# A gated linear unit over 8192 x 8192: two tiles to one store, and a load that waits for the tile before it

## The chip, the core and the metric

The kernel runs on one core of a Trainium2 chip. The metric is the device time of one execution in microseconds (us); the profile comes from one profiled execution, the times from separate ones. Transfers between HBM (the chip's large memory) and SBUF (the core's own memory of 128 partitions) are carried by 16 DMA engines, which serve the queues of all issuers: loads are issued by SyncE (SP), stores by ScalarE (ACT). VectorE (DVE), ScalarE and GpSimd (POOL) compute; TensorE has no work here.

## The reference

```python
# x: (8192, 8192) float32
a, b = np.split(x, 2, axis=-1)
return a * (1 / (1 + np.exp(-b)))     # (8192, 4096) float32
```

Of each row the first half is multiplied by the sigmoid of the second half. 268.4 MB are read and 134.2 MB written.

## The kernel before

**Tiles.** The 8192 rows are cut into 32 tiles of 256 rows. A tile puts R = 2 neighbouring rows into each of the 128 partitions: `x_g[i // 2, i % 2]` is a block in which partition p holds 2 x 8192 floats, 64 KB, that lie together in HBM. Two tiles with the same `i // 2` are interleaved: of four neighbouring rows the first two belong to the even tile, the last two to the odd one. So a tile's result is 2 x 4096 floats, 32 KB, in each partition, and the results of the two tiles of a pair together are 64 KB that lie together in HBM.

**Buffers.** SBUF has two slots for x (`xs`, 64 KB per partition each) and two for the result (`os`, 32 KB each); tile i uses slot `i % 2` of both.

**Work on a tile** (`work`). ScalarE writes sigmoid(b) over b in place (line 82); the product of a and that goes to the output slot (line 84). An ordinary tile is done in two pieces (`few_and_most`): 3/16 of the columns of both rows (1536 elements per partition), whose product is made by GpSimd, and the other 13/16 (6656 elements), whose product is made by VectorE. Tile 0 and tile 31 are done in four pieces of 2048 elements each (`fourths`), with products on VectorE alone, and tile 1 has both its products on VectorE.

**Order and waits.** The loop goes over the tiles: the two pieces of work, the load of tile i + 2, the store of tile i. Each engine runs its own instructions in this order. `place` drops every dependency on a tile's buffers but those named:

- a load waits for the products of the tile that had its x slot, two tiles back;
- a sigmoid waits for its load, and, in tiles 1 to 30, for the store that frees the output slot;
- a product waits for its sigmoid (in tile 31 for the freed output slot as well);
- a store waits for the products of its tile.

Tile 0 is loaded in two halves and stored in two halves; tile 31 is stored in pieces of a half, a quarter and a quarter. `_launch_early` puts the first load ahead of the start-up barrier, and `_close_on_sync` rewrites the end of the program so that only SyncE waits for the last store.

Of the kernel before, what the change touches and what calls it, by code (L numbers as in the profile page):

```python
# [8 lines left out]
def _tiles(ctx, tc, x, out):  # L9
    nc = tc.nc  # L10
    P = nc.NUM_PARTITIONS
    DEP = mybir.DependencyInfo(mybir.DependencyClass.Sync, mybir.DependencyReason.DATA)
    fp32 = mybir.dt.float32
    SIG = mybir.ActivationFunctionType.Sigmoid

    n_rows, n_cols = x.shape
    half = n_cols // 2
    R = 2
    SLOTS = 2
    n_tiles = n_rows // (P * R)  # L20
    x_g = x.rearrange("(g p h r) m -> g h p (r m)", p=P, h=2, r=R)
    out_g = out.rearrange("(g p h r) m -> g h p (r m)", p=P, h=2, r=R)

    pool = ctx.enter_context(tc.tile_pool(name="io", bufs=1))
    xs = [pool.tile([P, R * n_cols], fp32, name=f"x_sb{k}") for k in range(SLOTS)]
    os = [pool.tile([P, R * half], fp32, name=f"o_sb{k}") for k in range(SLOTS)]

    whole = [(0, 8)]
    rows = [(0, 4), (4, 8)]
    cut = half // 16 * 3  # L30
    few_and_most = [(0, 8, 0, cut), (0, 8, cut, half)]
    fourths = [(k, k + 2, k % 4 * half // 4, (k % 4 + 2) * half // 4) for k in range(0, 8, 2)]
    loads = [whole] * n_tiles
    works = [few_and_most] * n_tiles
    stores = [whole] * n_tiles
    behind = [0] * n_tiles
    loads[0] = stores[0] = rows
    works[0] = works[-1] = fourths
    stores[-1] = [(0, 4), (4, 6), (6, 8)]
    behind[-1] = 1  # L40

    def meet(a, b):
        return a[0] < b[1] and b[0] < a[1]

    traced = [[] for _ in range(SLOTS)]
    load_of, mul_of, store_of = {}, {}, {}

    def place(i, ins, *needs):


        kept = {n.ins.name for n in needs}
        for e in traced[i % SLOTS]:
            if e.ins.name not in kept:
                tc.declare_no_dep(ins.ins, e.ins, reason="follows from the waits that are kept")
        traced[i % SLOTS].append(ins)
        tc.keep_in_program_order(ins)
        return ins

    def load(i):
        for lo, hi in loads[i]:  # L60
            c = slice(lo * n_cols // 4, hi * n_cols // 4)
            free = [m for w, m in mul_of.get(i - SLOTS, []) if meet(w, (lo, hi))]
            ins = nc.sync.dma_start(out=xs[i % SLOTS][:, c], in_=x_g[i // 2, i % 2, :, c])  # L63
            load_of.setdefault(i, []).append(((lo, hi), place(i, ins, *free)))

    def store(i, lo, hi):
        c = slice(lo * half // 4, hi * half // 4)
        ins = nc.scalar.dma_start(out=out_g[i // 2, i % 2, :, c], in_=os[i % SLOTS][:, c])  # L68
        done = [m for w, m in mul_of[i] if meet(w, (lo, hi))]
        store_of.setdefault(i, []).append(((lo, hi), place(i, ins, *done)))  # L70

    def work(i, lo, hi, near, far):

        rows = xs[i % SLOTS].rearrange("p (r h m) -> p r h m", r=R, h=2)
        packed = os[i % SLOTS].rearrange("p (r m) -> p r m", r=R)
        r, c = slice(lo // 4, (hi + 3) // 4), slice(near, far)
        b = rows[:, r, 1, c]
        landed = [s for w, s in load_of[i] if meet(w, (lo, hi))]
        gone = [s for w, s in store_of.get(i - SLOTS, []) if meet(w, (lo, hi))]
        by_sigmoid = 0 < i < n_tiles - 1  # L80
        needs = [*landed, *(gone if by_sigmoid else ())]
        sig = place(i, nc.scalar.activation(out=b, in_=b, func=SIG), *needs)  # L82
        engine = nc.gpsimd if far == cut and i > 1 else nc.vector
        mul = engine.tensor_mul(out=packed[:, r, c], in0=rows[:, r, 0, c], in1=b)  # L84
        if by_sigmoid:
            for s in gone:
                tc.add_manual_dep(sig.ins, s.ins.name, DEP, reason="frees the output slot")
        place(i, mul, sig, *(() if by_sigmoid else gone))
        mul_of.setdefault(i, []).append(((lo, hi), mul))

    for i in range(SLOTS):
        load(i)
    for i in range(n_tiles):
        due = list(stores[i])
        for k, piece in enumerate(works[i]):
            work(i, *piece)
            ready = works[i][k - behind[i]][1] if k >= behind[i] else 0
            while len(stores[i]) > 1 and k < len(works[i]) - 1 and due[0][1] <= ready:
                store(i, *due.pop(0))
        if i + SLOTS < n_tiles:  # L100
            load(i + SLOTS)
        for lo, hi in due:
            store(i, lo, hi)


def _launch_early(nc):
# [68 lines left out]
@with_exitstack  # L175
def kernel(
    ctx: ExitStack,
    tc: tile.TileContext,
    x: bass.AP,
    out: bass.AP,  # L180
):
    nc = tc.nc
    with ExitStack() as pools:
        _tiles(pools, tc, x, out)
    tc.close()
    tc.compile()
    _launch_early(nc)
    _close_on_sync(nc)
# [30 lines left out]
```

## Time and profile before

| | before |
|---|---|
| median of 3 runs | 932.73 us (932.71 to 932.75) |
| profiled execution, first to last instruction (its span) | 931.1 us |
| between the span and the median | 1.6 us |
| VectorE busy | 232.5 us, 25% of the span, 39 multiplies |
| ScalarE busy | 229.8 us, 25%, 68 activations and a table load |
| GpSimd busy | 99.9 us, 11%, 29 multiplies and 4 memsets |
| sigmoids of an ordinary tile | 1.48 + 5.73 us |
| its products | GpSimd 3.44 us, VectorE 7.09 us |
| one load, issue to landing (median) | 43.5 us |
| one store, issue to landing (median) | 43.6 us |

The profiled execution's own time is its span of 931.1 us and what lies around it: the page gives no other time for it, and the runs stand 1.6 us above the span. In the profile's lines L63 is the load, L68 the store, L82 the sigmoid and L84 the product. In lines of the chain the columns are start, duration (both in us) and what ran; in the timeline they are start, busy time, engine, line, operation, buffers and shapes, count, and in brackets the idle time before it with what ended it; in a window they are the stretch, its length, the busy time of VectorE, ScalarE and GpSimd with their instructions, the TensorE clock, the share of the DMA engines and GB/s. Digits in the row of slices are tenths of a fortieth of the span, 9 being 90% or more.

### The profile page before, as it was taken

The numbers are of one execution on the slowest core, as the hardware profiler recorded it, in microseconds if no ns is written. First come the engines' busy times: TensorE is split into PE (matmuls) and PEld (weight loads), VectorE is DVE, ScalarE is ACT, GpSimd is POOL, SyncE is SP. The second block draws the span as 40 slices with busy tenths as digits, with TensorE's granted clock in tenths as the row PEclk, the third lists the DMA queues.
The fourth block names the chain that finished last, engine by engine and source line by source line (L and its number), as shares of the span: only waits on it lengthen the run. The fifth ranks groups of instructions, "written<-read, shape, count | busy, mean of one in ns | idle before, by whom it ended". The sixth has DMA issues, their size and how long they took to land.

```text
span 931.1 us, 325 instructions
## 1 busy us (share of the span) xinstructions
DVE 232.5 (25%) x39; ACT 229.8 (25%) x69; POOL 99.9 (11%) x33
## 2 busy tenths in 40 slices
DVE  1133311333113331133320333203332033320233
ACT  2123332033320333203332023320233302333023
POOL 0001111011110111101111011110111101111010
DMA  9999999999999999999999999999999999999998
GB/s 405 450 439 417 428 450 424 455 405 428 450 428 450 407 469 409 428 450 427 452 405 450 428 428 450 424 452 408 428 450 428 450 408 465 411 428 450 427 452 383
DMA packets 9793, 402.67 MB, mean 432 GB/s; under 512 B 1088, under 2 KB 1088, under 8 KB 1088
## 3 DMA queue, kind: packets, MB, share of 16 engines
q1 hardware_dynamic: 4752, 268.44, 66.6%
q10 hardware_dynamic: 5040, 134.22, 33.4%
q14 instruction: 1, 0.01, 0.0%
HBM read 268.44 MB, written 134.22 MB: 432 GB/s over the span
## 4 chain that ended last, share of the span: by engine, by line
DMA 75%; DVE 12%; ACT 12%; issue 0%; ACTq 0%; SPq 0%
DMA out_dram<-o_sb 65%; DVE o_sb L84 12%; ACT x_sb L82 12%; DMA x_sb<-in_x_dram 10%; ACTq L68 0%; SPq L63 0%
## 5 line engine op out<-in xcount | busy, mean ns | idle before, releaser
L84 DVE TENSOR_TENSOR o_sb<-x_sb 128x6656 f32<-128x6656 f32 (+2 forms) x39 | 232.5, 5970 | 690.2 <-ACT x_sb L82 690.2
L82 ACT ACTIVATE x_sb<-x_sb 128x1536 f32<-128x1536 f32 (+1 forms) x68 | 228.5, 3407 | 689.9 <-DMA out_dram<-o_sb 630.0
L84 POOL TENSOR_TENSOR o_sb<-x_sb 128x1536 f32<-128x1536 f32 x29 | 99.7, 3437 | 787.7 <-ACT x_sb L82 787.7
L82 ACT ACT_TABLE_LOAD x1 | 1.3, 1283 | 0.8 <-PEq L203 0.8
L203 POOL MEMSET const-float32-0.0<- 128x1 f32 x1 | 0.1, 98 | 0.2 <-issue 0.2
L203 POOL MEMSET const-bfloat16-1.0<- 128x1 bf16 x1 | 0.1, 101 | 0.0
L203 POOL MEMSET const-uint8-127<- 128x1 uint8 x1 | 0.1, 101 | 0.0
L203 POOL MEMSET const-float32-1.0<- 128x1 f32 x1 | 0.1, 98 | 0.0
## 6 DMA issues: line engine op xcount, KB each, us to landing
out_dram<-o_sb ACTq DMA_DIRECT2D x30, 4096.0 KB, 43.6
x_sb<-in_x_dram SPq DMA_DIRECT2D x2, 4096.0 KB, 16.4
out_dram<-o_sb ACTq DMA_DIRECT2D x3, 2048.0 KB, 28.0
out_dram<-o_sb ACTq DMA_DIRECT2D x2, 1024.0 KB, 8.3
x_sb<-in_x_dram SPq DMA_DIRECT2D x31, 43.5
```

Of the source, the lines that this page charges most:

```text
L82: sig = place(i, nc.scalar.activation(out=b, in_=b, func=SIG), *needs)
L84: mul = engine.tensor_mul(out=packed[:, r, c], in0=rows[:, r, 0, c], in1=b)
L203: nc = _bacc.Bacc("TRN2", target_bir_lowering=False, num_devices=1)
```

## The change

The two output slots become one buffer of 64 KB per partition (`packed`): the even tile writes its first half, the odd tile its second. Tiles 0 to 29 form 15 pairs, and each pair is written by one store of 64 KB per partition, issued after the odd tile's products. Tiles 30 and 31 keep stores of their own.

The waits change with it:

- the products of a pair's first tile wait for the store of the pair before, and so do those of tiles 30 and 31; no sigmoid waits for a store any more;
- the load of an odd tile from tile 3 on waits, besides the products that free its x slot, for the last sigmoid of the even tile before it; it is issued in that tile's turn, ahead of the load of the next even tile, which still waits for the products of the tile in its slot;
- tile 30's store is issued by itself, and tile 31's pieces follow as before: a half, a quarter, a quarter.

Pieces, engines and sizes of the computation stay. The core of the diff:

```diff
-    out_g = out.rearrange("(g p h r) m -> g h p (r m)", p=P, h=2, r=R)
+    out_g = out.rearrange("(g p k) m -> g p (k m)", p=P, k=2 * R)
...
-    os = [pool.tile([P, R * half], fp32, name=f"o_sb{k}") for k in range(SLOTS)]
+    packed = pool.tile([P, 2 * R * half], fp32, name="o_sb")
+    n_paired = n_tiles // 2 - 1
...
+    def is_paired(i):
+        return i < 2 * n_paired
...
+    def load(i, after=()):
+        for lo, hi in [(0, 4), (4, 8)] if i == 0 else [(0, 8)]:
             c = slice(lo * n_cols // 4, hi * n_cols // 4)
             ins = nc.sync.dma_start(out=xs[i % SLOTS][:, c], in_=x_g[i // 2, i % 2, :, c])
+            place(ins, mul_of.get(i - SLOTS, []), after)
             load_of.setdefault(i, []).append(((lo, hi), ins))
...
+    def store(i, lo, hi, done):
         c = slice(lo * half // 4, hi * half // 4)
+        ins = nc.scalar.dma_start(out=out_g[i // 2, :, c], in_=packed[:, c])
+        return place(ins, done)
...
-        sig = place(i, nc.scalar.activation(out=b, in_=b, func=SIG), *needs)
+        sig = place(nc.scalar.activation(out=b, in_=b, func=SIG), landed)
...
+        mul = place(engine.tensor_mul(out=o[:, r, c], in0=rows[:, r, 0, c], in1=b), [sig, *gone[i % 2]])
...
     for i in range(n_tiles):
+        first, last = i == 0, i == n_tiles - 1
+        for k, piece in enumerate(fourths if first or last else few_and_most):
             work(i, *piece)
+            if last and k == 2:
+                store(i, 8, 12, mul_of[i][:2])
+        if i % 2 == 0 and 0 < i + 1 - SLOTS:
+            if is_paired(i - 1):
+                load(i + 1, [sig_of[i][-1]])
+        if i + SLOTS < n_tiles and not (i % 2 and is_paired(i)):
             load(i + SLOTS)
+        if is_paired(i):
+            if i % 2:
+                s = store(i, 0, 16, mul_of[i - 1][-2:] + mul_of[i])
+                gone = [[s], [s]]
+            else:
+                gone[1] = []
+        elif not last:
+            gone[i % 2] = [store(i, i % 2 * 8, i % 2 * 8 + 8, mul_of[i])]
+    store(n_tiles - 1, 12, 14, mul_of[n_tiles - 1][2:3])
+    store(n_tiles - 1, 14, 16, mul_of[n_tiles - 1][3:])
```

More of the change, by code (lines that the diff above doesn't have):

```diff
@@ L21, in _tiles @@
     x_g = x.rearrange("(g p h r) m -> g h p (r m)", p=P, h=2, r=R)
-    out_g = out.rearrange("(g p h r) m -> g h p (r m)", p=P, h=2, r=R)
+    out_g = out.rearrange("(g p k) m -> g p (k m)", p=P, k=2 * R)
     pool = ctx.enter_context(tc.tile_pool(name="io", bufs=1))
     xs = [pool.tile([P, R * n_cols], fp32, name=f"x_sb{k}") for k in range(SLOTS)]
-    os = [pool.tile([P, R * half], fp32, name=f"o_sb{k}") for k in range(SLOTS)]
-    whole = [(0, 8)]
-    rows = [(0, 4), (4, 8)]
+    packed = pool.tile([P, 2 * R * half], fp32, name="o_sb")
+    n_paired = n_tiles // 2 - 1
     cut = half // 16 * 3
@@ L32, in _tiles @@
     fourths = [(k, k + 2, k % 4 * half // 4, (k % 4 + 2) * half // 4) for k in range(0, 8, 2)]
[L33 to L46, printed above, removed]
@@ L48, in place @@
-    def place(i, ins, *needs):
-        kept = {n.ins.name for n in needs}
-        for e in traced[i % SLOTS]:
+    def is_paired(i):
+        return i < 2 * n_paired
+    placed = []
+    sig_of, mul_of, load_of = {}, {}, {}
+    gone = [[], []]
+    def place(ins, needs, after=()):
+        kept = {n.ins.name for n in (*needs, *after)}
+        for e in placed:
             if e.ins.name not in kept:
                 tc.declare_no_dep(ins.ins, e.ins, reason="follows from the waits that are kept")
-        traced[i % SLOTS].append(ins)
+        for n in (*needs, *after):
+            tc.add_manual_dep(ins.ins, n.ins.name, DEP, reason="kept")
+        placed.append(ins)
@@ L56, in place @@
         tc.keep_in_program_order(ins)
         return ins
-    def load(i):
-        for lo, hi in loads[i]:
+    def load(i, after=()):
+        for lo, hi in [(0, 4), (4, 8)] if i == 0 else [(0, 8)]:
             c = slice(lo * n_cols // 4, hi * n_cols // 4)
-            free = [m for w, m in mul_of.get(i - SLOTS, []) if meet(w, (lo, hi))]
             ins = nc.sync.dma_start(out=xs[i % SLOTS][:, c], in_=x_g[i // 2, i % 2, :, c])
-            load_of.setdefault(i, []).append(((lo, hi), place(i, ins, *free)))
@@ L66, in store @@
-    def store(i, lo, hi):
+            place(ins, mul_of.get(i - SLOTS, []), after)
+            load_of.setdefault(i, []).append(((lo, hi), ins))
+    def store(i, lo, hi, done):
         c = slice(lo * half // 4, hi * half // 4)
-        ins = nc.scalar.dma_start(out=out_g[i // 2, i % 2, :, c], in_=os[i % SLOTS][:, c])
-        done = [m for w, m in mul_of[i] if meet(w, (lo, hi))]
-        store_of.setdefault(i, []).append(((lo, hi), place(i, ins, *done)))
+        ins = nc.scalar.dma_start(out=out_g[i // 2, :, c], in_=packed[:, c])
+        return place(ins, done)
@@ L72, in work @@
     def work(i, lo, hi, near, far):
         rows = xs[i % SLOTS].rearrange("p (r h m) -> p r h m", r=R, h=2)
-        packed = os[i % SLOTS].rearrange("p (r m) -> p r m", r=R)
+        o = packed.rearrange("p (h r m) -> p h r m", h=2, r=R)[:, i % 2]
         r, c = slice(lo // 4, (hi + 3) // 4), slice(near, far)
         b = rows[:, r, 1, c]
-        landed = [s for w, s in load_of[i] if meet(w, (lo, hi))]
-        gone = [s for w, s in store_of.get(i - SLOTS, []) if meet(w, (lo, hi))]
-        by_sigmoid = 0 < i < n_tiles - 1
@@ L81, in work @@
-        needs = [*landed, *(gone if by_sigmoid else ())]
-        sig = place(i, nc.scalar.activation(out=b, in_=b, func=SIG), *needs)
-        engine = nc.gpsimd if far == cut and i > 1 else nc.vector
[L84 to L89, printed above, removed]
+        landed = [s for w, s in load_of[i] if w[0] < hi and lo < w[1]]
@@ L91, in _tiles @@
+        sig = place(nc.scalar.activation(out=b, in_=b, func=SIG), landed)
+        engine = nc.gpsimd if far == cut and i > 1 else nc.vector
+        mul = place(engine.tensor_mul(out=o[:, r, c], in0=rows[:, r, 0, c], in1=b), [sig, *gone[i % 2]])
+        sig_of.setdefault(i, []).append(sig)
+        mul_of.setdefault(i, []).append(mul)
     for i in range(SLOTS):
@@ L93, in _tiles @@
     for i in range(n_tiles):
-        due = list(stores[i])
-        for k, piece in enumerate(works[i]):
+        first, last = i == 0, i == n_tiles - 1
+        for k, piece in enumerate(fourths if first or last else few_and_most):
             work(i, *piece)
[L97 to L100, printed above, removed]
-            load(i + SLOTS)
-        for lo, hi in due:
-            store(i, lo, hi)
+            if last and k == 2:
[4 more added lines that the diff above has]
+        if i + SLOTS < n_tiles and not (i % 2 and is_paired(i)):
+            load(i + SLOTS)
+        if is_paired(i):
[8 more added lines that the diff above has]
+    store(n_tiles - 1, 14, 16, mul_of[n_tiles - 1][3:])
 def _launch_early(nc):
```

## The prediction

> **What bounds the kernel now.** I read the page from the top: engines, then slices, then DMA queues.
>
> ```profile
> span 931.1 us, 325 instructions
> ...
> DMA  9999999999999999999999999999999999999998
> ...
> DMA packets 9793, 402.67 MB, mean 432 GB/s; under 512 B 1088, under 2 KB 1088, under 8 KB 1088
> ...
> q1 hardware_dynamic: 4752, 268.44, 66.6%
> q10 hardware_dynamic: 5040, 134.22, 33.4%
> ```
>
> The 16 DMA engines are busy in every slice; VectorE and ScalarE, the busiest engines, stand at 25% of the span. q1 (loads) and q10 (stores) add up to 100.0%, so bytes bound the kernel. The counts also give the packets: 33 loads of 128 rows are 4224, 16 small ones per load make 4752. The 35 stores give 4480 + 560 = 5040. So a load packet is one row of 64 KB, a store packet one of 32 KB.
>
> Next, the chain of waits over one tile, the timeline of the next, and one window of 29 us.
>
> ```profile
> 99.66 7.13 ACT x_sb L82 x2
> 106.79 0.02 issue
> 106.81 7.10 DVE o_sb L84
> ...
> 113.99 43.64 DMA out_dram<-o_sb
> 157.63 0.02 issue
> 157.66 7.13 ACT x_sb L82 x2
> ```
>
> ```profile
> 128.66 7.12 ACT L82 ACTIVATE x_sb<-x_sb 128x1536 f32<-128x1536 f32 x2 [21.88 <-DMA out_dram<-o_sb]
> 130.22 3.44 POOL L84 TENSOR_TENSOR o_sb<-x_sb 128x1536 f32<-128x1536 f32 x1 [25.56 <-ACT x_sb L82]
> 135.81 7.09 DVE L84 TENSOR_TENSOR o_sb<-x_sb 128x6656 f32<-128x6656 f32 x1 [21.91 <-ACT x_sb L82]
> 142.99 0.35 ACTq L68 DMA_DIRECT2D out_dram<-o_sb  x1
> ```
>
> ```profile
> 99.66:128.66 29.00, 7.09 (x1) 7.12 (x3) 3.44 (x1) 1.00 1.00 434
> ```
>
> A tile takes 29.0 us, in which 8.39 MB are loaded and 4.19 MB stored: 434 GB/s. The chain runs through stores, but a store's 43.6 us are queueing: 14.6 behind the store before it, 29.0 for itself. In the 29.0 us a load moves twice the bytes, so packets of 64 KB and of 32 KB alternate. Both queues always hold work, so nothing the compute engines do is seen. GpSimd's multiply ends at 133.66, VectorE's begins at 135.81: they never run together.
>
> **What the change moves.** Bytes and engine instructions stay the same; stores go from 35 to 19. The only possible gains are cheaper packets; the only losses are stretches with empty queues.
>
> *Fewer, longer store packets.* In the trace's packet records 64 KB take 2.418 us and 32 KB take 1.213 us, so joining two saves 2 x 1.213 - 2.418 = 0.008 us. Each engine joins 8 rows per pair, in 15 pairs: 120 x 0.008 = 0.96. Neighbouring packets overlap by a few ns, so I take 0.9 us of gain. Issue instructions saved (16 of 0.36 us) lie beside transfers: nothing.
>
> *Start and end.* The first store is issued some 37 us later (18.45 before, near 55.7 by the steps below), but loads fill that time. At the end only stores remain in both versions, with the same last piece sizes: nothing.
>
> *The new order in a pair.* Call the tiles A and B, the next pair's A' and B', then A''. One tile's load, alone, takes 8.39 MB / 434 GB/s = 19.3 us, and so does a pair's store. With 64 KB packets in both queues they now share by halves, not 2:1. "l" is the time from an issue to its first packet, taken as equal for every transfer. Count from B's last packet; A' is queued behind B:
>
> 1. B: landing 0.4 (last packet to sigmoid), sigmoids 7.13, multiply 7.10, issue 0.04: the store is issued at 14.7, first packet at 14.7 + l. A' then has 4.6 - l to go, and shares.
> 2. A' lands; sigmoids 0.4 + 7.13; only then is B' issued, first packet l later. The store runs alone for 7.5 + l and has 19.3 - (4.6 - l) - (7.5 + l) = 7.2 left. This is the cover of the new wait: the queues don't run dry there unless sigmoids and issue take 7 us more. Behind the waiting load on SP's queue stands only A'', which must wait longer anyway.
> 3. Store and B' share; the store ends 14.4 us later, and B' has 19.3 - 7.2 = 12.1 left. **These 12.1 us are all the cover there is.**
> 4. The multiplies of A' wait for the whole store, as they overwrite its buffer. A'' needs the x slot of A', so it waits for both multiplies. From the store's last packet: landing 0.6 (99.10 to 99.66 in the trace), VectorE 7.10, then l: 7.7 + l. If GpSimd's 3.44 us come on top: 11.2 + l. ACT's queue holds the store of the pair and behind it the sigmoids of a tile that lands later; GpSimd and VectorE hold B's multiplies behind A's, and B has not landed: no further loss.
>
> So the queues stand empty for c = 7.7 + x + l - 12.1 = x + l - 4.4, if positive. Two costs in it are shown by no row.
>
> x, the price of both multiplies being released by one store: between 0 and 3.44 us (the serial end). A gain is excluded: an operation gets no shorter by having company. I take 3.44: the nearest rows have the two strictly one after the other, both read the same x tile and write the same buffer, and no row shows a free overlap.
>
> The Trainium skill (SBUF — State Buffer, "Who interferes with whom") says that a VectorE instruction with two SBUF inputs and a GpSimd instruction that reads SBUF exclude each other for a whole instruction; by this rule x is 3.44 too and the sum is the one below. This trace has no overlap to test it on.
>
> l: the very first load shows its first packet 1.01 us after issue, with idle engines; the first store (issued at 18.45, first packet at 23.58) took 5.13 beside a running load. Those are the ends. Of the 5.13 one running packet of 2.42 may be waiting for a turn, which a load behind its own queue doesn't pay: I take 5.13 - 2.42 = 2.7.
>
> c = 3.44 + 2.7 - 4.4 = 1.7 us. An empty stretch delays A'' by as much, so more of it is shared with the next store, and the next cover grows by that stretch: the next gap is c minus this one. On average c/2. The loads of tiles 4, 6, ... 30 are exposed, 14 in all: 14 x 0.85 = 12 us. **Sum: +12 - 0.9 = +11 us.**
>
> Bounds: x = 3.44 and l = 1.01 give c = 0.05, nothing; l = 5.13 gives c = 4.2 and +29 us. x = 0 gives no gap up to l = 4.4 and +5 us at l = 5.13, less the 0.9. Sharing goes in steps of 2.4 us, which can move any of these by some us.
>
> The profiled span is 931.1, the median of three runs 932.73; I carry the 1.6 us between them over. 932.7 + 11 = 944 (span 942.4).
>
> **Rivals.**
>
> *Not slower: the two multiplies run side by side.* Then x = 0, A'' is issued 7.7 after the store, in the queue at 10.4, and 12.1 of cover suffice. What decides is x: below 4.4 - l = 1.7 nothing is lost. For it: GpSimd's 3.44 us would lie wholly inside VectorE's 7.10, and ScalarE beside either costs nothing today. Against it: no row has the pair together. Time: 932.7 - 0.9 = 931.8. Chance 0.17.
>
> *Not slower: prompt issue.* Even serial multiplies fit if l is at most 0.96. The first load's 1.01 nearly does; the first store's 5.13 speaks against it. 931.8 to 932.5, chance 0.11. The Trainium skill (DMA: Bandwidth & Descriptors, "Latency and other measured facts") puts the first byte of such a transfer at about 0.6 us; by it the gap vanishes and the sum is 931.8. The trace agrees in the first load's order of size and disagrees in the first store.
>
> *Slow issue alone.* x = 0 but l near 5: c = 0.7, +4 us, 937. Chance 0.03.
>
> *The store doesn't do what it says.* If its rows still left as 32 KB packets, the store would get a third of the engines beside a load: 8.2 us left at step 3 take 24.6, B' has 2.9 left against 13.9 needed, c = 11, some 77 us lost, about 1009. Loads of 64 KB rows do travel as one packet, so 0.02.
>
> **How the numbers follow.** The forecast has 0.62. This kernel's measurements tell 0.2% (1.9 us) from no change. Slower: 0.62 + 0.03 + 0.02 = 0.67. Same: the two not-slower rivals, 0.28. Faster by over 1.9 us would need twice the packet saving that the records give, with no gap at all: 0.05. The range goes down to the not-slower cases, 931 (931.8, with up to 1 us for the steps of sharing), and up to 957: c = 3.7, near the bound l = 5.13. In the forecast's own case it is 936 to 957.
>
> **What would show it.** Right: after each pair's store lands, GpSimd's and VectorE's multiplies of the even tile start together and the later ends 10.5 us on; the next load is issued some 11 us after the landing; DMA slices of 8 and GB/s below 434; VectorE or GpSimd in the chain ahead of a load. Wrong: the multiplies end 7.1 us after the landing, and the DMA digits stay at 9; or stores with 256 packets per pair; or an empty stretch elsewhere, such as between a store's end and the held load.

## The result, and the profile after

| | before | changed |
|---|---|---|
| median of 5 runs | 932.73 us (932.69 to 935.17) | 970.68 us (967.71 to 971.82) |
| ratio to before | | 1.0399, 95% interval 1.0382 to 1.0415 |
| profiled execution: span | 931.1 us | 966.0 us (own time 967.71 us) |

The change costs 38 us, 4%. The prediction had 944, 931 to 957: right in direction, far off in size. The span grew by 34.9 us, and that growth is accounted for below. The profiled execution is the shortest of the five; the 3 us by which the median lies above it stand in no trace.

The page of the changed kernel, the lines that answer to those of before:

```profile
span 966.0 us, 311 instructions
...
DMA  9999999999999999999999999999999999999999
...
DMA packets 7490, 402.67 MB, mean 417 GB/s; under 512 B 832, under 2 KB 832, under 8 KB 832
...
q1 hardware_dynamic: 4752, 268.44, 66.6%
q10 hardware_dynamic: 2736, 134.22, 32.1%
```

The row of nines says nothing. The two queue lines say nearly all. Together they hold 98.7% of the span, so the engines were empty for 1.3% of 966 us, some 12.6 us; before, the two lines held 100.0%. And the loads, with the same bytes and the same 4752 packets, still take 66.6% of a span that is 35 us longer: 0.666 x 966.0 = 643 us instead of 0.666 x 931.1 = 620 us. Load packets became slower by 23 us. Stores did not: 310 us against 311. 2736 packets are 19 stores of 128 + 16, so rows of 64 KB do leave as one packet.

The chain of waits over two pairs, from one store's landing to the next but one (start, duration, what):

```profile
88.58 10.33 POOL o_sb L71
98.93 25.36 DMA x_sb<-in_x_dram
...
131.51 29.16 DMA x_sb<-in_x_dram
...
175.03 31.95 DMA out_dram<-o_sb
...
207.11 10.33 POOL o_sb L71
```

and the timeline at the head of it, with two windows, each from one store's landing to the next:

```profile
88.54 7.09 DVE L71 TENSOR_TENSOR o_sb<-x_sb 128x6656 f32<-128x6656 f32 x1 [33.22 <-DMA out_dram<-o_sb]
88.58 10.32 POOL L71 TENSOR_TENSOR o_sb<-x_sb 128x1536 f32<-128x1536 f32 x1 [88.14 <-DMA out_dram<-o_sb]
...
102.07 3.43 POOL L71 TENSOR_TENSOR o_sb<-x_sb 128x1536 f32<-128x1536 f32 x1 [3.17 <-ACT x_sb L69]
107.67 7.09 DVE L71 TENSOR_TENSOR o_sb<-x_sb 128x6656 f32<-128x6656 f32 x1 [12.04 <-ACT x_sb L69]
```

```profile
88.44:148.56 60.12, 14.18 (x2) 14.24 (x4) 13.76 (x2) 1.00 1.00 419
148.56:206.98 58.42, 14.18 (x2) 14.24 (x4) 13.76 (x2) 1.00 0.98 413
```

GpSimd's product takes 3.43 us in the odd tile, where it runs by itself, and 10.32 us in the even tile, where the store releases it with VectorE's: it ends 3.27 us after VectorE. GpSimd now stands in the chain, ahead of a load; before it did not appear there. The load of the next even tile is issued at 98.93, 10.5 us after the landing, and by then the queues are running dry: by the packet records the engines finish the load before it one after another between 99.16 and 100.16, and the next load's first packet starts at 99.89.

**Where 34.9 us went.** The trace's packet records have the start, the duration and the size of every packet. From them two sums can be made, each divided by 16 engines: time in which an engine runs no packet ("empty"), and what packets last beyond their usual 2.418 us for 64 KB, 1.213 for 32 KB and so on ("stretched"). In the changed kernel there are 12.7 us more of empty time than before, and 22.7 us more of stretched packets, of which some 8 us in the first load packets after an empty stretch (about 0.65 us each time) and some 14 us in the last load packets ahead of a store that joins (0.7 to 1.3 us each time, mostly some 3.6 us a packet instead of 2.4). 12.7 + 22.7 = 35.4; the span grew by 34.9, and the remaining -0.5 us is what the longer store packets save. The same sums close for every kernel that was run:

| kernel | span against before | empty | stretched | rest |
|---|---|---|---|---|
| changed kernel | +34.9 | +12.7 | +22.7 | -0.5 |
| even tiles without GpSimd products | +2.3 | +0.4 | +2.5 | -0.5 |
| even tiles all on VectorE | +31.0 | +6.9 | +24.6 | -0.5 |
| pair stores in the load queue | +9.2 | +4.6 | +5.2 | -0.5 |
| no hold | +111.8 | +84.9 | +27.3 | -0.5 |
| hold alone, 32 KB stores | +56.8 | +34.7 | +22.0 | +0.1 |
| GpSimd products in two even tiles | +9.5 | +3.0 | +7.1 | -0.5 |
| hold behind VectorE's product | +269.6 | +241.4 | +28.7 | -0.5 |
| before, with one late load | +9.3 | +7.2 | +2.1 | +0.1 |
| hold longer by 3.4 us | +11.4 | +2.3 | +9.6 | -0.5 |
| hold longer by 1.9 us | +10.5 | +0.9 | +10.0 | -0.5 |

### The profile page after: what moved, and what is told of

The parts are those of the page before. It is cut to its first block, busy times and chain, and to the rows that moved or that the text cites. A ratio compares the mean times of both kernels' runs of the same rounds, so it can differ in the third digit from the quotient of the medians.

```text
span 966.0 us, 311 instructions
## 1 busy us (share of the span) xinstructions
DVE 232.5 (24%) x39; ACT 229.8 (24%) x69; POOL 203.2 (21%) x33
## 3 DMA queue, kind: packets, MB, share of 16 engines
q1 hardware_dynamic: 4752, 268.44, 66.6%
q10 hardware_dynamic: 2736, 134.22, 32.1%
## 4 chain that ended last, share of the span: by engine, by line
DMA 73%; ACT 11%; POOL 7%; DVE 7%; issue 0%; SPq 0%; ACTq 0%; POOLq 0%
DMA x_sb<-in_x_dram 47%; DMA out_dram<-o_sb 26%; ACT x_sb L69 11%; POOL o_sb L71 7%; DVE o_sb L71 7%; SPq L54 0%; ACTq L60 0%; POOLq L71 0%
## 5 line engine op out<-in xcount | busy, mean ns | idle before, releaser
L71 POOL TENSOR_TENSOR o_sb<-x_sb 128x1536 f32<-128x1536 f32 x29 | 203.0, 7000 | 737.8 <-DMA out_dram<-o_sb 683.2
```

The costliest lines, as they stand in the source:

```text
L71: mul = place(engine.tensor_mul(out=o[:, r, c], in0=rows[:, r, 0, c], in1=b), [sig, *gone[i % 2]])
```

## The experiments

Three theories at the outset. **A**: two separate costs, the empty stretches that hang on the late products, and a price of 1.1 us for every store that joins the loads. **B**: one cause, the late products; no empty stretch, no stretched packets. **C**: the sharing by halves and the hold are to blame, and the products are incidental.

### Even tiles without GpSimd's products

```diff
+        if far == cut and i > 1 and i % 2 == 0:
+            return
         engine = nc.gpsimd if far == cut and i > 1 else nc.vector
```

(The odd tile's products then wait for the store themselves, which has landed by then.)

> Leaves out GpSimd's products in even tiles from tile 2 on: 3/16 of the columns of those tiles keep older values. So only VectorE's product (7.09 us) follows the store, and the load of the next even tile should be issued 7.1 us after the landing, not 10.4. In the changed kernel's trace the 34.9 us of longer span are 12.7 us of empty DMA engines, 8.3 us of load packets stretched right after such an empty stretch, and 14.3 us of load packets stretched when a store joins. Theory A (two costs: the empty stretches hang on the products, the stretch at a store's joining belongs to the pair store itself): only the last remains, 932.7 + 14 = 947 us. Theory B (one cause, the late products; the joining costs nothing by itself): about 932 us. Theory C (sharing by halves and the held load are to blame, the products don't matter): 965 us or more.

Measured: 935.29 us, ratio 1.0029 (1.0019 to 1.0038). This decides for B. The first two lines are from its page, the others from its timeline:

```profile
q1 hardware_dynamic: 4752, 268.44, 66.7%
q10 hardware_dynamic: 2736, 134.22, 33.3%
...
146.87 7.09 DVE L74 TENSOR_TENSOR o_sb<-x_sb 128x6656 f32<-128x6656 f32 x1 [32.08 <-DMA out_dram<-o_sb]
153.99 0.33 SPq L54 DMA_DIRECT2D x_sb<-in_x_dram  x1
```

The two queues hold 100.0% of 933.4 us, and the loads are back at 622 us. With VectorE's 7.09 us alone behind the store the next load is issued in time, no stretch is empty between the first and the last pair, and the 15 stores join nearly free: only the very first has stretched packets ahead of it (1.19 us). C falls: sharing by halves and the hold are both still there. A falls with its 947. B's 932 is missed by some 3 us, of which the records give 2.5 us as stretched packets.

### Even tiles all on VectorE

```diff
-        engine = nc.gpsimd if far == cut and i > 1 else nc.vector
+        engine = nc.gpsimd if far == cut and i > 1 and i % 2 else nc.vector
```

(Here too, and in the kernel with GpSimd's products in two even tiles, the odd tile's products wait for the store themselves.)

> The whole product of an even tile on VectorE, 1.76 + 7.09 = 8.85 us after the store's landing instead of 10.4 with GpSimd behind VectorE. Theory A: between 947 and 970, some 955 us, since the empty stretches shrink but the joining stays. Theory B: between 932 and 970, with the stretch at joining shrinking in the same proportion as the empty stretches. Theory C: 965 us or more.

Measured: 963.76 us, ratio 1.0331 (1.0316 to 1.0347). The nearest to a dose between 7.1 and 10.4 us. The empty time halved, 6.9 us instead of 12.7, but the stretched packets stayed, 24.6 instead of 22.7. Behind its shortest stretches, of 0.2 to 0.3 us, the first load packets cost 0.5 to 0.65 us and the last ones ahead of the next store 1.0 to 1.5; behind its longest, of 1.3 us, 0.6 and 1.1. In this range what counts is that the queues run dry, not for how long. Nor is it GpSimd's product that stretches the packets: in even tiles there is none here. So the second half of B, that both shrink in proportion, was wrong.

### Pair stores in the load queue

```diff
+        queue = nc.sync if hi - lo == 16 else nc.scalar
+        ins = queue.dma_start(out=out_g[i // 2, :, c], in_=packed[:, c])
```

> The pair's store is issued by SyncE, in the same queue as the loads, so it never joins beside them: it follows the load in flight and the held load follows it. The held load then covers 19.3 us behind the store, against 0.6 + 10.4 + 1.0 us until the next load: no empty queue. Theory A: neither cost is left, 932 us, perhaps 931. Theory B: 932 us too. Theory C (64 KB packets in stores or the late products cost by themselves): 945 us or more.

Measured: 943.03 us, ratio 1.0109 (1.0094 to 1.0124), so above the 932 of A and B and below C. Two windows of its trace, one pair and a stretch of the end:

```profile
839.70:897.80 58.10, 14.19 (x2) 14.24 (x4) 13.77 (x2) 1.00 1.00 431
924.00:930.00 6.00, 5.52 (x3) 4.66 (x4) 0.00 (x0) 1.00 0.21 87
```

The pair takes 58.1 us, twice the 29.0 of before, with GpSimd at 10.3 us: the order in one queue covers the late products. 4.8 us are lost at the end: tile 31's load has landed by 922.5, tile 30's store, issued at 908.81, runs out on most engines by 924, and the first piece of tile 31 is issued only at 929.00. The rest are stretched packets. One of these tells something more. The first store is preceded by packets stretched by 1.22 us here too, though it stands in the loads' own queue. So a second queue is not needed for the stretch. It is not the change from loading to storing by itself either: the other 14 pair stores of this run have no such group ahead of them.

### No hold

```diff
-                load(i + 1, [sig_of[i][-1]])
+                load(i + 1)
```

> The odd tile's load no longer waits for the even tile's sigmoids. Theories A and B: the store now shares the DMA engines by halves for its whole length, some 38 us instead of 32, so the even tile's products and the next load come later, and the two loads ahead of them have long landed: some 5 us lost per pair more than in the changed kernel, 1010 to 1030 us. Rival (the hold is what costs): below 965 us.

Measured: 1044.22 us, ratio 1.1192 (1.1175 to 1.121), a little above the range given. Sharing with loads for its whole length, the store lands late, and nearly every pair has an empty stretch of 5 to 6 us (the first 9.9). The hold is not a cost in the changed kernel; it is what keeps the loss at 4% instead of 12%.

### The hold alone

The changed kernel with every tile stored by itself again:

```diff
-            if i % 2:
-                s = store(i, 0, 16, mul_of[i - 1][-2:] + mul_of[i])
-                gone = [[s], [s]]
-            else:
-                gone[1] = []
+            gone[i % 2] = [store(i, i % 2 * 8, i % 2 * 8 + 8, mul_of[i])]
```

> One part alone: the held load stays, but every tile is stored by itself again, 32 KB per partition, as soon as its products are done. An even tile's products then wait only for the store of the even tile before, which has long landed, so the next even tile's load is issued 14.3 us after the tile's landing and not 0.6 + 10.4 us after a pair's store. Theory B (the late products run the queues dry): no dry stretch there; what is left is the hold itself, some 7.5 + 1 us in which only a 32 KB store of 9.7 us runs: 932 to 940 us. Rival (the hold costs by itself): above 950 us.

Measured: 991.01 us, ratio 1.0632 (1.061 to 1.0655). A miss, and on the rival's side of 950: I had the 32 KB store run alone through the hold for its whole 9.7 us. The trace has it issued at 124.77, with its first row leaving at 130.05, while a load still runs, and landed at 142.88. The load queue, empty from 134.9 on, gets the held load only at 142.87: the queues are dry for 1.7 us in most pairs, and the packets behind and ahead are stretched as in the changed kernel (0.6 and 0.7 us each time). Here it is the hold that runs the queues dry, not the late products. Either part alone costs more, 58 us for the hold and 112 for the shared store, than both together.

### GpSimd's products in two even tiles

```diff
-        if far == cut and i > 1 and i % 2 == 0:
+        if far == cut and i > 1 and i % 2 == 0 and i not in (8, 20):
```

(Against the kernel whose even tiles have no GpSimd products.)

> As the kernel whose even tiles have no GpSimd products (935.3 us), but with them in tiles 8 and 20 only; in the other even tiles from tile 2 on 3/16 of the columns keep older values. Theory B' (each dry stretch pays three times: empty engines about 0.9 us, the first load packets after it stretched by 0.65, and the last load packets ahead of the next store stretched by 1.15): these three are seen behind tile 8's and tile 20's products and nowhere else but at the first store, and the time is up to 2 x 2.7 us longer, 935 to 941 us. Theory A (a store's joining costs 1.1 us by itself): no stretch that goes with the two tiles.

Measured: 941.79 us, ratio 1.0095 (1.0079 to 1.0112). Four windows, one to a pair, taken within 0.6 us of the stores' landings; tile 8's products lie at the start of the third:

```profile
146.80:204.90 58.10, 14.18 (x2) 14.24 (x4) 3.44 (x1) 1.00 1.00 432
204.90:263.00 58.10, 14.19 (x2) 14.24 (x4) 3.44 (x1) 1.00 1.00 433
263.60:324.30 60.70, 14.19 (x2) 14.24 (x4) 13.76 (x2) 1.00 0.98 415
324.30:382.00 57.70, 14.19 (x2) 14.24 (x4) 3.44 (x1) 1.00 1.00 435
```

The pair with GpSimd's late product is the one that is longer. From one landing to the next, by the starts of VectorE's products behind them (147.06, 205.44, 263.67, 324.42, 382.66), it takes 60.8 us and the others 58.2 to 58.4, so it is longer by 2.4 to 2.5 us. In the packet records the three parts stand behind tile 8 and again behind tile 20: empty 1.3 and 0.8 us, the first load packets stretched by 0.55 and 0.68, the load packets ahead of the next store by 1.12 and 1.11, together 2.9 and 2.6. Of the other stores only the first of the kernel has such packets ahead of it; some 2 us of stretched packets elsewhere go with neither. This is the clearest of the runs: the late product, the dry queue and the stretched packets go together, pair by pair.

### A longer hold, wrongly placed

VectorE, meant to be idle, multiplies 128x3328 elements into a spare buffer behind the sigmoids, and the odd tile's load waits for that.

> The whole computation, and the odd tile's load is held longer: VectorE, idle there, multiplies 128x3328 elements into a spare buffer (about 3.6 us) after the even tile's sigmoids, and the load waits for that. By the balance of the prediction each us of hold leaves the store one us less to share and the held load one us more of cover, so 3.6 us more should take c from about +1 to about -2.6: no dry stretch, no stretched packets but at the first store, about 935 us, with GpSimd still behind VectorE at 10.3 us. Rival (a later load just makes everything later): 970 us or more.

Measured: 1202.13 us, ratio 1.289 (1.2871 to 1.2909). My mistake: VectorE runs in order, and the spare multiply stood behind the even tile's product, which waits for the whole store. So the held load waited for the products too, and it and the load of the next even tile were issued together, at 94.88. One thing in its timeline is worth more than the time:

```profile
81.00 7.09 DVE L72 TENSOR_TENSOR o_sb<-x_sb 128x6656 f32<-128x6656 f32 x1 [25.76 <-DMA out_dram<-o_sb]
81.05 10.33 POOL L72 TENSOR_TENSOR o_sb<-x_sb 128x1536 f32<-128x1536 f32 x1 [80.61 <-DMA out_dram<-o_sb]
88.01 6.84 DVE L87 TENSOR_TENSOR spare<-x_sb 128x3328 f32<-128x3328 f32 x1
```

VectorE's 3328 elements would take half of its 7.09 us for 6656, some 3.55 us. They took 6.84 and ended at 94.85, 3.47 us after GpSimd's product: now VectorE waited some 3.3 us for GpSimd. In both orders that these runs show, the multiply that comes second waits for the first to end.

### The longer hold on ScalarE

```diff
+                more = place(nc.scalar.activation(out=spare, in_=xs[i % SLOTS][:, :3840], func=SIG), sig_of[i][-1:])
+                load(i + 1, [more])
```

> The whole computation, and the hold longer by a spare activation of 128x3840 on ScalarE (3.3 to 3.5 us) behind the even tile's sigmoids; the odd tile's load waits for it. By the balance one us of hold takes one us from c, as one us less of products after the store does. So 3.4 us more hold should do what leaving out GpSimd's 3.3 us did: no dry stretch, some 935 us, with GpSimd still at 10.3 us behind VectorE. Rival (a later load only makes what follows later): 970 us or more.

Measured: 942.97 us (938.57 to 944.63), ratio 1.0104 (1.0077 to 1.013).

```profile
129.20 3.40 ACT L86 ACTIVATE spare<-x_sb 128x3840 f32<-128x3840 f32 x1
132.68 19.50 SPq L55 DMA_DIRECT2D x_sb<-in_x_dram  x2
141.46 7.09 DVE L72 TENSOR_TENSOR o_sb<-x_sb 128x6656 f32<-128x6656 f32 x1 [26.99 <-DMA out_dram<-o_sb]
141.50 10.33 POOL L72 TENSOR_TENSOR o_sb<-x_sb 128x1536 f32<-128x1536 f32 x1 [36.28 <-DMA out_dram<-o_sb]
```

With the whole computation, GpSimd still at 10.33 us and 3.4 us of extra waiting, 28 of the 38 us are gone: a later load makes the kernel faster, as the balance says. No stretch is empty before 680 us and hardly any after, up to one of 2.3 us at the end. It stays 8 us above the 935 expected, mostly in stretched packets of the later pairs (9.6 us in all). These come where the queues do not run dry, or hardly: the last five pair stores have 0.55 to 0.8 us of stretched load packets ahead of them, behind at most 0.17 us of empty time and in one pair behind none. So a dry stretch is not the whole condition.

### The hold longer by half as much

The same with 128x2048 elements.

> The same with a spare activation of 128x2048 (1.9 us). By the balance this is worth about as much as the product on VectorE alone (1.5 us less after the store: 963.8 us): dry stretches shorter but still in most pairs, 950 to 962 us. Rival as above: 970 us or more.

Measured: 950.84 us (943.12 to 957.1), ratio 1.0218 (1.0182 to 1.0253), inside what was given, and in order between 970.68 and 942.97, but its runs spread over 14 us. Its profiled execution was its shortest and shows only 0.9 us more of empty time, with 10.0 us of stretched packets, so it says nothing of the longer ones.

### One late load in the kernel before

Tile 16's load is issued in tile 15's turn, ahead of tile 17's, and waits for tile 15's products (the lines that move it are not shown):

```diff
+            if i == 16:
+                tc.add_manual_dep(ins.ins, mul_of[15][-1][1].ins.name, DEP, reason="one late load")
```

> The kernel before, with one load late: tile 16's waits for tile 15's products instead of tile 14's, once. Queues then hold only a store of 9.7 us after tile 15's load has landed, against 14.6 us of work on tile 15 and 1 us to the first packet: the engines stand empty for some 5.8 us. If an empty stretch costs only itself: 932.6 + 5.8 = 938.4 us. Theory B' (the restart costs more): first load packets stretched by 0.65 us and perhaps 1.15 us at the store behind: 939 to 940.5 us.

Measured: 942.23 us, ratio 1.0107 (1.0092 to 1.0122), 9.7 us more and above the 939 to 940.5 given: the empty time came out at 7.2 us instead of 5.8, and 2.1 us are stretched packets: 1.3 us in the first load packets after the stop and 0.6 about the next transfer that joins. So in this kernel without pairs, too, the one stop cost some 2 us beyond itself.

No version here beats the kernel before.

## Why the prediction was right or wrong

**"Both queues always hold work" (before) and the order of a pair (steps 1 to 4): right.** The A'' load waits as described, and 7.10 + 3.44 = 10.54 us of multiplies were 10.49 from landing to issue. The sizes within the steps are another matter (below).

**x = 3.44, the serial end: right.** 3.27 us, fifteen times over, and the reverse case in the wrongly placed hold. The first rival, the products side by side, is thereby refuted; leaving GpSimd out of even tiles shows about what it would have brought, 935. The rule of the Trainium skill that was set beside this (SBUF — State Buffer, "Who interferes with whom": the second to issue is blocked until the first ends) agrees with the trace: 10.32 us, of which VectorE's are 7.09.

**l = 2.7 for every transfer: wrong.** The load on a nearly dry queue shows its first packet 0.96 us after issue (98.93 to 99.89), the held load beside a running store 3.84 (71.17 to 75.01), a store beside a running load 5.2 (55.35 to 60.52). Over all pairs the held loads show 3.4 to 4.7 us and the pair stores 3.2 to 6.1. The second rival, prompt issue, had its l of 0.96 and still lost, since the transfers before it were late. The Trainium skill gives about 0.6 us to the first byte (DMA: Bandwidth & Descriptors, "Latency and other measured facts"). Counted from the end of the issue instruction, which lasts 0.33 us here, the 0.96 agree with it; the transfers beside running ones don't.

**14 x c/2 = 12 us of empty queues: right in sum, and partly by luck.** Measured 12.7, in 12 of the 14 places and at the end, on average 0.85 us a place, as forecast. But the gaps do not go as c minus the one before: the first six are 0.5, 0.35, 0, 1.6, 0.2 and 1.1 us. Their terms are off as well. A store ends with a 4-byte packet on each engine, and this goes 2.4 us after the engine's last row, behind one more load packet, a turn that the steps don't have. From these packets' mean time A'' needs 13.4 us to its issue, not 11.1, because the landing is that of the last engine; B' then has 14.1 us left, not 12.1; and the first packets of A'' start 1.6 us after its issue, not 2.7. These errors cancel.

**"The only losses are stretches with empty queues": this is the step that failed.** I took 2.418 us for every load packet and priced a dry queue at its empty time. In the changed kernel a dry queue costs about 2.7 us: some 0.95 empty, 0.65 in the first load packets behind it, 1.15 in the last ones ahead of the next store. The two missing terms are the 22.7 us of stretched packets, and they are most of the error: the span grew by 34.9 us, 23.8 more than the 11.1 of the sum. The trace of before held a hint: its only store to join after loads alone, the one issued at 18.45, had load packets of up to 2.86 us ahead of it.

**The packets' saving of 0.9: right in sign, too large.** The rest in the table is -0.5 us in all nine kernels with 64 KB stores and +0.1 in the two with 32 KB. Rows and closing packets together do last some 1.2 us less, but packets overlap their neighbours by less, too: 1.6 us in all, against 2.2 before.

**Start and end at nothing: two small costs.** At the end engines are empty for 0.8 us (between 954.1 and 956.5), where tile 30's store runs out before tile 31's pieces are under way; and the first store has 1.1 us of stretched load packets ahead of it, against some 0.25 about the first store of before.

**The signs.** Both multiplies start with the landing, the later ends 10.5 us on, GpSimd stands in the chain and GB/s fell to 417: as said. But the DMA digits stayed at 9, which had been named with the signs of being wrong: gaps of about 1 us are too short for slices of 24 us.

**Open:** why packets are stretched after a dry stretch, and ahead of the store that follows. The records show that the packets ahead of a first store are stretched with one queue as with two, and that in the changed kernel the others go with dry stretches; with the longer holds some are stretched where the queues hardly ran dry. They show no mechanism.

## What to carry to other kernels

In a kernel at the limit of its transfers, count for each buffer that is freed late what is still queued when the next transfer can be issued, and keep a margin of some us: in these runs a queue that just ran dry paid again for its restart: in the changed kernel 1.3 to 1.4 us behind 0.2 to 0.3 us of empty time, and 1.9 to 2.0 behind 1.6. Sum the time of the queues' packets, not only the gaps: the same bytes with a longer queue time are a loss that a row of nines hides. When one event releases two engines, cost their work in series until a trace shows otherwise.

## What the runs showed that was not expected

- GpSimd's and VectorE's multiplies, each with two inputs in SBUF, run one after the other, in either order: 10.32 us instead of 3.43 for GpSimd behind VectorE, 6.84 instead of some 3.55 for VectorE behind GpSimd.
- After a dry stretch of 0.2 to 1.6 us, the first load packets of the changed kernel last 2.7 to 3.2 us and the last ones before the next store mostly 3.3 to 3.7, against 2.418; its store packets keep their time.
- A longer wait ahead of a load took 28 us off: 970.68 to 942.97.
